# Adding up a paired tile's seven products in PSUM, with two of the four weight sums and the right factors' sums moved from GpSimd to VectorE

## The chip, the core and the metric

The kernel runs on one core of one Trainium2 chip. The metric is device time in microseconds (us): the median of several executions of the same program. Five engines share the work: TensorE (PE in the profile; its weight loads are PEld), VectorE (DVE), ScalarE (ACT), GpSimd (POOL) and SyncE (SP), which issues the DMAs. Each engine works through its own queue in order; semaphores tie the queues together. Matrix products land in PSUM, in eight banks; everything else lives in SBUF.

## What is computed

One decoder layer for 512 prompt tokens and 32 sample tokens, T = 544 columns in all: a half-step SwiGLU feed-forward block, a mixer (block-sparse attention and a gated linear recurrence side by side), and a second half-step SwiGLU block. The change touches the two feed-forward blocks.

```python
x = x + 0.5 * swiglu(rms_norm(x, ffn1_norm), ffn1_gate, ffn1_up, ffn1_down)
h = rms_norm(x, mix_norm); z = h @ w_in          # split among head groups
x = x + concat(moba(q, k, v), gate * norm(hgrn2(q, f, i))) @ w_out
x = x + 0.5 * swiglu(rms_norm(x, ffn2_norm), ffn2_gate, ffn2_up, ffn2_down)
```

Here swiglu(x) = (silu(x @ gate) * (x @ up)) @ down, with 1024 model columns and 2816 hidden columns.

## The kernel before

**Layout.** Activations are kept transposed: eight tiles `x[0..7]` of 128 model columns by 544 tokens. `HT` = 272 is half of the tokens, and every large matrix product is 128 by 128 by 272. Each operand is split into a high part, a cast to the format that TensorE takes at full pace (fp32r), and a low part, the remainder; a product is three matmuls, high by high, high by low and low by high (`products`). So every weight tile costs an ACT cast (`whi`) and a DVE subtraction (`wlo`), which `split_unit` issues. When a raw slot or a slot for split weights is taken from elsewhere, these appear under names such as `xh` and `xl`.

**Stages.** A feed-forward block has 22 hidden tiles in three groups (`FGROUPS`: 8, 8 and 6). For each group `ffn` first makes the hidden tiles and then adds their share of the down projection, eight output tiles. Below they are called groups A, B and C.

**Plain and paired tiles.** The first `NREG` = 4 hidden tiles are plain: gate and up are two products each over eight k-tiles and two token halves, 96 matmuls per hidden tile. They read `xg`, which needs no norm factor `R`, so that they can start early. From the fifth tile on, gate and up are made together. The four quarters of their weights (a11, a12: gate, first and second half of k; a21, a22: up) and the four quarters of the normed activations are combined by Winograd's form of Strassen's scheme: seven products instead of eight, 84 matmuls per hidden tile. It needs

- four weight sums per tile, S0 = a21 + a22, S1 = S0 - a11, S2 = a11 - a21, S3 = a12 - S1, which `w_split` issues on POOL,
- seven right factors per k-pair (`right_factors`, run as a side chain once per block as soon as `R` exists): two products on DVE, four sums of 272 columns on POOL, and four splits on ACT and DVE,
- the results added up from the seven products. `paired_gemm` gives each product its own bank out of three (`mm`), and `hidden_paired` takes them in: two are copied by ACT (`s1`, `s5`, in the tile `t_g`), five are added to an SBUF operand by DVE (into `sq`, `t_s`, `t_h`), and two further sums of SBUF operands go to POOL (`late`). ACT applies silu twice; one DVE product over 544 columns and the split of the hidden tile (`hh`, `hl`) end the tile.

**What sets the order.** The whole program is planned before anything is emitted. `Order` keeps a model of each engine's time; the backbone (the PE stream) and side chains are generators, and every instruction gets a planned start. `fit` puts an instruction of DVE, ACT or POOL into the first free gap of that engine's modelled time, also behind the current moment, and each engine's queue is then emitted in the order of planned starts (`give_out`). The durations in `cost` are a rough model; the real ones come from the trace.

**Weights.** `w_pump` splits weight tiles as long as a slot is free, and loads raw tiles as long as a raw slot is free. `next_w` hands units to the PE stream in the order in which they were split, which for a paired tile is a11, S0, S1, S2, a12, S3, a22. Four slots of each kind always exist; during the paired tiles `more_slots` lends four more raw and six more split ones.

Of the kernel before, what the change touches and what calls it, by code (L numbers as in the profile page):

```python
# [14 lines left out]
AF = mybir.ActivationFunctionType  # L15
ALU = mybir.AluOpType
# [11 lines left out]
HT = T // 2  # L28
# [22 lines left out]
OVER, TICK, WARM_COLUMNS = 0.0112, 3.413, 3060  # L51
NREG = 4
WARM = 10
# [123 lines left out]
class Engine:  # L177
# [22 lines left out]
    def __getattr__(self, op):  # L200
        real = getattr(self.real, op)

        def call(*args, **kw):
            names = list(self.tensors(args, kw))
            if op == "dma_start":
                s = self.order.dma(self.part, 4 * args[1].shape[0] * self.free(args[1]), names)
            elif op == "indirect_dma_start":
                s = self.order.dma(self.part, 4 * args[0].shape[0] * self.free(args[0]),
                                   names + [args[3].ap.tensor.name], 1.0)
            else:  # L210
                s = self.order.spend(self.part, self.cost(op, args, kw), names, op)
            self.order.note(s, real, args, kw)

        return call

    def cost(self, op, args, kw):
# [27 lines left out]
class Order:  # L244
# [4 lines left out]
    def __init__(self):  # L249
        self.free = {"pe": 0.0}  # L250
        self.busy = {part: [] for part in ("dve", "act", "pool", "sp", "dma")}
        self.written, self.touched, self.slots, self.work, self.before = {}, {}, {}, {}, {}
# [35 lines left out]

    def fit(self, part, s, cost):

        q = self.busy[part]
        if len(q) > 400:
            del q[:200]
        if q:
            s = max(s, q[0][0])
        i = len(q)
        while i and q[i - 1][1] > s:
            i -= 1
        while i < len(q) and q[i][0] < s + cost:
            s = max(s, q[i][1])  # L300
            i += 1
        q.insert(i, (s, s + cost))
        return s
# [11 lines left out]

    def spend(self, part, cost, names, op):
        s = self.start(part, names)
# [75 lines left out]
class Build:  # L393
# [123 lines left out]
    def w_split(self):  # L517
# [10 lines left out]
        if job["paired"]:  # L528
            (a11, a12, a21, a22) = (r for r, _ in job["raw"])
            if n == 0:  # L530
                S = [self.tl(self.sums, [128, 4, 128], f"S{i}") for i in range(4)]
                for i, (p, q, op) in enumerate(((a21, a22, ALU.add), (S[0], a11, ALU.subtract),
                                                (a11, a21, ALU.subtract), (a12, S[1], ALU.subtract))):
                    self.nc.gpsimd.tensor_tensor(S[i][:, :nk], p[:, :nk], q[:, :nk], op=op)
                job["units"] = (a11, S[0], S[1], S[2], a12, S[3], a22)
            src = job["units"][n]
            self.units.append(self.split_unit(src, nk, x))
            drop = {0: (0, 2), 4: (1,), 6: (3,)}.get(n, ())
        else:
# [10 lines left out]
    def w_pump(self):  # L550
        while self.w_split() or self.w_load():
            pass
# [32 lines left out]

    def products(self, ps, w, k, xh, xl, first, last):
        hi, lo, _ = w
        for i, (ww, xx) in enumerate(((hi, xh), (hi, xl), (lo, xh))):
            self.nc.tensor.matmul(ps[:, :HT], ww[:, k], xx, start=first and i == 0, stop=last and i == 2)

# [28 lines left out]

    PAIRED = (0, 3, 4, 5, 1, 2, 6)  # L620

    def paired_gemm(self, xw, nk, evacs):


        for r, evac in zip(self.PAIRED, evacs):
            w, = self.next_w(1)
            ps = self.mm()
            for k in range(nk):
                xh, xl = xw[k]
                self.products(ps, w, k, xh[:, r], xl[:, r], k == 0, k == nk - 1)  # L630
                yield
            evac(ps[:, :HT])
            self.free_w([w])

    def right_factors(self, pool, x, gain):
# [6 lines left out]

        def pace(t):
            self.order.t = self.order.free["pe"] + t

        def split(hi, lo, r, src):
            nc.scalar.copy(hi[:, r], src)
            nc.vector.tensor_tensor(lo[:, r], src, hi[:, r].bitcast(F32), op=ALU.subtract)

        for k in range(n):  # L650
# [4 lines left out]
            lo = self.tl(pool, [128, 7, HT], f"xwl{k}", F32R)  # L655
            for B, m in ((B1, k), (B2, k + n)):
                nc.vector.scalar_tensor_tensor(B.rearrange("p a b -> p (a b)"), x[m],
                                               self.gains[:, gain, m:m + 1], self.R, op0=ALU.mult, op1=ALU.mult)
                pace(1.2)
# [4 lines left out]
            split(hi, lo, slice(0, 1), B1[:, 0:1])  # L664
            pace(1.2)
            yield
            split(hi, lo, slice(1, 3), B2)
            pace(1.2)
            yield
            split(hi, lo, slice(3, 5), S1)  # L670
            pace(1.2)
            yield
            split(hi, lo, slice(5, 7), S2)
            self.xw.append((hi, lo))
            pace(1.2)
            yield

# [107 lines left out]
    def hidden_paired(self, pool, i, hs):  # L785
# [6 lines left out]
        l, r = self.cols(0), self.cols(1)  # L792
        s1, s5, u2, u3 = p[:, l], p[:, r], q[:, l], q[:, r]
        add = lambda out, x, y: nc.vector.tensor_tensor(out, x, y, op=ALU.add)
        late = lambda out, x, y: nc.gpsimd.tensor_tensor(out, x, y, op=ALU.add)
# [9 lines left out]
        def p2(x):  # L805
            add(s[:, l], x, s1)
            nc.scalar.activation(s[:, l], s[:, l], AF.Silu)

        def p3(x):
            add(s[:, r], x, s[:, r])  # L810
            nc.scalar.activation(s[:, r], s[:, r], AF.Silu)

        def p4(x):
            add(u[:, l], x, u3)
            nc.vector.tensor_tensor(u, u, s, op=ALU.mult)
            hs[i] = self.split_hidden(u, i)

        return lambda x: nc.scalar.copy(s1, x), lambda x: nc.scalar.copy(s5, x), p6, p7, p2, p3, p4


# [140 lines left out]
    def load_x(self, pool, p, x):  # L961
# [17 lines left out]
        self.loading = self.splitting = 0  # L979
        self.units = []  # L980
        self.slots = {"raw": [{"pool": self.wp, "tags": ("raw",), "bufs": 4, "used": 0, "freed": [], "extra": None}],
                      "w": [{"pool": self.wp, "tags": ("whi", "wlo"), "bufs": 4, "used": 0, "freed": [], "extra": None}]}
# [851 lines left out]
```

## Time and profile before

| | us |
|---|---|
| median of 3 executions | 1233.71 |
| lowest, highest | 1231.61, 1234.82 |
| the profiled execution's own time | 1229.04 |
| its span, first to last instruction | 1227.3 |

| stretch of the profiled span | from, to (us) |
|---|---|
| start, plain tiles of the first block | 0 to 73.2 |
| first block: paired tiles of groups A, B, C | 73.2 to 127.8, 177.9 to 270.0, 317.8 to 382.5 |
| mixer | about 382 to 838 |
| second block: plain tiles | about 838 to 883.8 |
| second block: paired tiles of groups A, B, C | 883.8 to 933.5, 981.3 to 1069.7, 1117.6 to 1182.3 |
| last down projection and output | to the end |

How to read the profile: a row of the windows view gives a stretch, its length, and then for each engine how long it was busy and with how many instructions, and the granted share of TensorE's clock (PEclk). A row of the timeline gives the start and the length of an instruction, then its engine, operation and tiles (out<-in), shapes and, in square brackets, the idle time of the engine before it and what ended that. All instructions are recorded by one helper, so every row names the same line of the code (L274); the tiles tell them apart. Durations of neighbours on one engine overlap slightly, since the next one starts while the last is draining; the distance from start to start is what a queue pays.

### The profile page before, as it was taken

How to read it: one execution, taken by the hardware profiler on the slowest of the kernel's cores; microseconds unless marked ns; L12 is line 12 of the kernel's file. 1: busy time of each engine (PE TensorE's matmuls, PEld its weight loads, DVE VectorE, ACT ScalarE, POOL GpSimd, SP SyncE). 2: the span in 40 equal slices, each digit the busy share in tenths (PEclk: the TensorE clock that was granted, in tenths of full speed). 3: DMA queues.
4: the chain of work that ended last, by engine and by line, in shares of the span. 5: the costliest groups of instructions: out<-in, count | busy, mean ns of one | idle time of the engine just before them, and what ended most of it. 6: DMA issues, size and time to landing. Idle time of an engine off the chain costs nothing. (4 is left out here: it accounts for less than half of the span.)

```text
span 1227.3 us, 26588 instructions
## 1 busy us (share of the span) xinstructions
PE 1184.0 (96%) x10547; PEld 1114.1 (91%) x10547; DVE 911.0 (74%) x1671; ACT 544.0 (44%) x1103; POOL 473.3 (39%) x391
## 2 busy tenths in 40 slices
PE   8969999999999999999999999899889999999998
PEld 8969998999999998888878877799889999999998
DVE  6999649993796678888777457668897499937953
ACT  5445324542454426554556432344453255514532
POOL 3367118750662331000233344122573277505710
PEclk8999999999999999999999999899999999999999
DMA  5233353242313551432565786332433323332222
GB/s 161 73 105 99 107 160 96 85 118 82 89 55 98 169 181 56 129 87 70 182 193 166 231 275 234 132 111 71 119 98 110 95 79 95 110 89 78 65 84 81
DMA packets 216239, 144.74 MB, mean 118 GB/s; under 512 B 12035, under 2 KB 204067, under 8 KB 216116
## 3 DMA queue, kind: packets, MB, share of 16 engines
q1 hardware_dynamic: 205588, 106.60, 30.1%
q0 software_dynamic: 10432, 36.32, 9.0%
q8 instruction: 83, 1.36, 0.4%
q14 instruction: 40, 0.33, 0.1%
q10 hardware_dynamic: 96, 0.14, 0.0%
HBM read 133.94 MB, written 11.83 MB: 119 GB/s over the span
## 5 line engine op out<-in xcount | busy, mean ns | idle before, releaser
L274 PE MATMUL mm<-xh,whi 128*128 128x272 f32 x1152 | 346.4, 301 | 1.5 <-ACT xh L274 1.0
L274 PE MATMUL mm<-xh,wlo 128*128 128x272 f32 x1152 | 334.1, 290 | 5.0 <-DVE wlo L274 5.0
L274 PE MATMUL mm<-xl,whi 128*128 128x272 f32 x1152 | 333.9, 290 | 5.0 <-DVE xl L274 4.9
L274 ACT CAST whi<-raw 128x512 fp32r<-128x512 f32 (+1 forms) x224 | 135.3, 605 | 241.4 <-PE mm L274 182.9
L274 PEld LDWEIGHTS mm<-xh,whi 128*128 128x128 f32 x1152 | 218.8, 190 | 18.7 <-issue 16.0
L274 DVE TENSOR_TENSOR wlo<-raw,whi 128x512 fp32r<-128x512 f32 (+1 forms) x224 | 172.0, 775 | 73.5 <-ACT whi L274 69.7
L274 PEld LDWEIGHTS mm<-xl,whi 128*128 128x128 f32 x1152 | 219.3, 190 | 6.2 <-DVE xl L274 6.1
L274 PEld LDWEIGHTS mm<-xh,wlo 128*128 128x128 f32 x1152 | 218.9, 190 | 6.1 <-DVE wlo L274 6.1
L274 PE MATMUL mm<-xwh,xh 128*128 128x272 f32 x624 | 184.3, 295 | 10.8 <-DVE sq L274 7.8
L274 PE MATMUL mm<-xwl,xh 128*128 128x272 f32 x624 | 181.4, 291 | 0.0
L274 PE MATMUL mm<-xwh,xl 128*128 128x272 f32 x624 | 181.4, 291 | 0.0
L274 PEld LDWEIGHTS mm<-xwh,xh 128*128 128x128 f32 x624 | 119.4, 191 | 15.8 <-DVE sq L274 10.1
L274 PEld LDWEIGHTS mm<-xwl,xh 128*128 128x128 f32 x624 | 119.4, 191 | 0.0
L274 PEld LDWEIGHTS mm<-xwh,xl 128*128 128x128 f32 x624 | 119.2, 191 | 0.0
L274 PE MATMUL mm<-xwh,whi 128*128 128x272 f32 x384 | 112.4, 293 | 5.9 <-ACT t_g L274 2.7
L274 POOL TENSOR_TENSOR S<-raw,raw 128x512 f32<-128x512 f32 x28 | 42.0, 1500 | 189.5 <-DMA raw<-ffn_up 184.2
L274 PE MATMUL mm<-xwh,wlo 128*128 128x272 f32 x384 | 110.6, 288 | 3.1 <-DVE wlo L274 3.1
L274 PE MATMUL mm<-xwl,whi 128*128 128x272 f32 x384 | 110.3, 287 | 0.0
L274 PE MATMUL mm<-hl,whi 128*128 128x272 f32 x352 | 101.4, 288 | 0.0
L274 PE MATMUL mm<-hh,whi 128*128 128x272 f32 x352 | 101.2, 288 | 0.0
L274 PE MATMUL mm<-hh,wlo 128*128 128x272 f32 x352 | 101.2, 288 | 0.0
L274 DVE TENSOR_TENSOR xl<-S,xh 128x512 fp32r<-128x512 f32 x88 | 94.5, 1075 | 4.0 <-ACT xh L274 2.6
(308 smaller groups left out, 2439.4 us busy)
## 6 DMA issues: line engine op xcount, KB each, us to landing
raw<-ffn_down SPq DMA_DIRECT2D x64, 256.0 KB, 2.8
raw<-ffn_up SPq DMA_DIRECT2D x60, 256.0 KB, 3.0
raw<-w_in SPq DMA_DIRECT2D x56, 256.0 KB, 3.1
raw<-ffn_gate SPq DMA_DIRECT2D x48, 256.0 KB, 3.2
xh<-ffn_gate SPq DMA_DIRECT2D x24, 256.0 KB
raw<-ffn_down SPq DMA_DIRECT2D x32, 192.0 KB, 2.5
xl<-ffn_up SPq DMA_DIRECT2D x18, 256.0 KB, 2.9
xl<-ffn_gate SPq DMA_DIRECT2D x16, 256.0 KB, 3.3
```

Of the source, the lines that this page charges most:

```text
L274: call(*map(real, args), **{k: real(v) for k, v in kw.items()})
```

## The change

**Sums in PSUM.** A paired tile now owns three banks a, b and d, alternately from the `mm` and the `sm` banks (`self.turn`). The first three products open the three banks; the other four are added by TensorE onto what is there (`start=False` throughout). Between them VectorE adds `s1` to bank b in place. In order:

1. P1 into a; ACT copies it to `s1`
2. P6 into b; DVE adds `s1` to b in PSUM, ACT copies the result to `u2`
3. P5 into d; ACT copies it to `s5`
4. P2 onto a; ACT applies silu straight from the bank
5. P7 onto b; DVE writes b + `s5` to the right half of `t_h`
6. P3 onto d; DVE adds `u2`, ACT applies silu, DVE multiplies the right half (272 columns) of `t_h`
7. P4 onto b; DVE multiplies it with the left silu, and the hidden tile is split

The four additions that VectorE made on the way are now two (to b, and of `u2`) plus one (`s5`); the two sums on POOL are gone.

**Sums moved.** S0 and S1 go from POOL to DVE, S2 and S3 stay; the units' order becomes a11, S1, S0, a12, S2, S3, a22. In `right_factors` all four sums per k-pair go from POOL to DVE, each as a step of its own with a pause of 0.8 in the planner's time (`PACE`).

**Planner.** `NREG` is 5: one more tile is plain. A weight tile is split only while fewer than `AHEAD` = 4 are waiting at that point of the plan. DVE instructions with two larger SBUF operands and all POOL instructions but memsets now also reserve a common resource `port` in the plan.

```diff
-NREG = 4
+NREG = 5
+AHEAD = 4
+PACE = 0.8
...
+    def shares_port(self, op, args, kw):
+        if self.part not in ("dve", "pool") or op == "memset":
+            return False
+        n = sum(hasattr(x, "tensor") and self.free(x) > 1 and x.tensor.name[:2] not in ("mm", "sm")
+                for x in args[1:] if hasattr(x, "shape"))
+        return self.part == "pool" or n > 1
...
-            s = self.fit(part, s, cost)
+            s = self.fit([part, "port"] if port else part, s, cost)
...
-                for i, (p, q, op) in enumerate(((a21, a22, ALU.add), (S[0], a11, ALU.subtract),
-                                                (a11, a21, ALU.subtract), (a12, S[1], ALU.subtract))):
-                    self.nc.gpsimd.tensor_tensor(S[i][:, :nk], p[:, :nk], q[:, :nk], op=op)
-                job["units"] = (a11, S[0], S[1], S[2], a12, S[3], a22)
+                for i, (e, p, q, op) in enumerate(((self.nc.vector, a21, a22, ALU.add),
+                                                   (self.nc.vector, S[0], a11, ALU.subtract),
+                                                   (self.nc.gpsimd, a11, a21, ALU.subtract),
+                                                   (self.nc.gpsimd, a12, S[1], ALU.subtract))):
+                    e.tensor_tensor(S[i][:, :nk], p[:, :nk], q[:, :nk], op=op)
+                job["units"] = (a11, S[1], S[0], a12, S[2], S[3], a22)
...
-        while self.w_split() or self.w_load():
+        while (len(self.units) < AHEAD and self.w_split()) or self.w_load():
...
-    PAIRED = (0, 3, 4, 5, 1, 2, 6)
+    PAIRED = ((0, 0, True), (1, 4, True), (2, 3, True), (0, 1, False), (1, 5, False), (2, 2, False), (1, 6, False))
...
-        for r, evac in zip(self.PAIRED, evacs):
+        self.turn = not self.turn
+        ps = [self.mm() if self.turn else self.sm() for _ in range(3)]
+        views = [p[:, :HT] for p in ps]
+        for (b, r, first), evac in zip(self.PAIRED, evacs):
             w, = self.next_w(1)
-            ps = self.mm()
             for k in range(nk):
                 xh, xl = xw[k]
-                self.products(ps, w, k, xh[:, r], xl[:, r], k == 0, k == nk - 1)
+                self.products(ps[b], w, k, xh[:, r], xl[:, r], first and k == 0, k == nk - 1, not first)
                 yield
-            evac(ps[:, :HT])
+            evac(*views)
             self.free_w([w])
...
-            for out, p, q in ((S1[:, 0], B1[:, 1], B1[:, 0]), (S1[:, 1], B2[:, 1], S1[:, 0]),
-                              (S2[:, 0], B2[:, 1], B1[:, 1]), (S2[:, 1], B2[:, 0], S1[:, 1])):
-                nc.gpsimd.tensor_tensor(out, p, q, op=ALU.subtract)
...
+            steps += [lambda a=a: diff(*a) for a in ((S1[:, 0], B1[:, 1], B1[:, 0]), (S1[:, 1], B2[:, 1], S1[:, 0]),
+                                                     (S2[:, 0], B2[:, 1], B1[:, 1]), (S2[:, 1], B2[:, 0], S1[:, 1]))]
...
+            for step in steps:
+                step()
+                self.order.t = self.order.free["pe"] + PACE
                 yield
...
-        def p6(x):
-            add(u2, x, s1)
-            late(s[:, r], u2, s5)
-
-        def p7(x):
-            add(u3, x, u2)
-            late(u[:, r], u3, s5)
...
+        def p6(a, b, d):
+            add(b, b, s1)
+            nc.scalar.copy(u2, b)
+
+        def p3(a, b, d):
+            add(g, d, u2)
+            silu(s[:, r], g)
+            nc.vector.tensor_tensor(u[:, r], u[:, r], s[:, r], op=ALU.mult)
+
+        def p4(a, b, d):
+            nc.vector.tensor_tensor(u[:, l], b, s[:, l], op=ALU.mult)
             hs[i] = self.split_hidden(u, i)
...
+        return (lambda a, b, d: nc.scalar.copy(s1, a), p6, lambda a, b, d: nc.scalar.copy(s5, d),
+                lambda a, b, d: silu(s[:, l], a), lambda a, b, d: add(u[:, r], b, s5), p3, p4)
```

**What moves on VectorE.** The rows below are VectorE's queue in the fourth paired tile of group B of the first block, before: one tile's worth of rows from the sum of P6 (`sq` from a bank `mm` and `t_g`) on. A row is an operation, out<-in and its shape; `xl` and `wlo` from a raw tile or an `S` are weight remainders, `hl` is that of the hidden tile.

```order
L274 TENSOR_TENSOR sq_515_2744<-mm_2718,t_g_2700 128x272
L274 TENSOR_TENSOR xl_525_2755<-S_499_2628,xh_524_2741 128x512
L274 TENSOR_TENSOR sq_515_2744<-mm_2738,sq_515_2744 128x272
L274 TENSOR_TENSOR xl_528_2775<-raw_2475,xh_527_2766 128x512
L274 TENSOR_TENSOR t_s_2753<-mm_2763,t_g_2700 128x272
L274 TENSOR_TENSOR xl_536_2798<-raw_2439,xh_535_2790 128x512
L274 TENSOR_TENSOR t_s_2753<-mm_2787,t_s_2753 128x272
L274 TENSOR_TENSOR wlo_2819<-S_531_2672,whi_2811 128x512
L274 TENSOR_TENSOR t_h_2773<-mm_2808,sq_515_2744 128x272
L274 TENSOR_TENSOR t_h_2773<-t_h_2773,t_s_2753 128x544
L274 TENSOR_TENSOR wlo_2845<-S_532_2703,whi_2832 128x512
L274 TENSOR_TENSOR hl_544_2860<-t_h_2773,hh_543_2848 128x544
```

The same tile after the change, from the addition into bank b on:

```order
L284 TENSOR_TENSOR mm_2637<-mm_2637,t_g_2641 128x272
L284 TENSOR_TENSOR xl_484_2667<-xl_414_2275,xh_483_2647 128x512
L284 TENSOR_TENSOR xl_494_2676<-S_471_2565,xh_493_2661 128x512
L284 TENSOR_TENSOR S_500_2686<-raw_2530,raw_2593 128x512
L284 TENSOR_TENSOR xl_496_2697<-S_472_2590,xh_495_2690 128x512
L284 TENSOR_TENSOR S_501_2706<-S_500_2686,raw_2435 128x512
L284 TENSOR_TENSOR t_h_2726<-mm_2637,t_g_2641 128x272
L284 TENSOR_TENSOR xl_498_2730<-xh_437_2444,xh_497_2710 128x512
L284 TENSOR_TENSOR sq_458_2670<-mm_2658,sq_458_2670 128x272
L284 TENSOR_TENSOR t_h_2726<-t_h_2726,t_s_2704 128x272
L284 TENSOR_TENSOR t_h_2726<-mm_2637,t_s_2704 128x272
L284 TENSOR_TENSOR xl_505_2771<-raw_2435,xh_504_2723 128x512
```

The next tile's two weight sums (`S_500`, `S_501`) now stand in VectorE's queue just ahead of the row that reads bank b after the fifth product (`t_h` from `mm` and `t_g`); the row that multiplies `t_h` by the second silu follows right behind the row that feeds that silu (`sq`).

**What moves on GpSimd.** Its queue for one tile there before (the sums of the next tile, and the two sums `t_s` and `t_h` of this one):

```order
L274 TENSOR_TENSOR S_496_2517<-xh_452_2436,raw_2475 128x512
L274 TENSOR_TENSOR S_497_2548<-S_496_2517,xh_432_2341 128x512
L274 TENSOR_TENSOR S_498_2572<-xh_432_2341,xh_452_2436 128x512
L274 TENSOR_TENSOR t_s_2598<-sq_480_2589,t_g_2545 128x272
L274 TENSOR_TENSOR t_h_2618<-sq_480_2589,t_g_2545 128x272
L274 TENSOR_TENSOR S_499_2628<-xl_433_2278,S_497_2548 128x512
```

and after, for three tiles in a row:

```order
L284 TENSOR_TENSOR S_471_2565<-xh_413_2334,xl_423_2381 128x512
L284 TENSOR_TENSOR S_472_2590<-xl_414_2275,S_470_2557 128x512
L284 TENSOR_TENSOR S_502_2714<-raw_2435,raw_2530 128x512
L284 TENSOR_TENSOR S_503_2739<-raw_2483,S_501_2706 128x512
L284 TENSOR_TENSOR S_533_2863<-xh_475_2632,xl_485_2679 128x512
L284 TENSOR_TENSOR S_534_2888<-xl_476_2584,S_532_2855 128x512
```

Six rows per tile have become two.

More of the change, by code (lines that the diff above doesn't have):

```diff
@@ L210, in call @@
             else:
-                s = self.order.spend(self.part, self.cost(op, args, kw), names, op)
+                s = self.order.spend(self.part, self.cost(op, args, kw), names, op, self.shares_port(op, args, kw))
             self.order.note(s, real, args, kw)
         return call
+    def shares_port(self, op, args, kw):
[4 more added lines that the diff above has]
+        return self.part == "pool" or n > 1
     def cost(self, op, args, kw):
@@ L250, in __init__ @@
         self.free = {"pe": 0.0}
-        self.busy = {part: [] for part in ("dve", "act", "pool", "sp", "dma")}
+        self.busy = {part: [] for part in ("dve", "act", "pool", "sp", "dma", "port")}
         self.written, self.touched, self.slots, self.work, self.before = {}, {}, {}, {}, {}
@@ L287, in born, with fit @@
         q.append(name)
[L289 to L302, printed above, removed]
+    def fit(self, parts, s, cost):
+        parts = [parts] if isinstance(parts, str) else parts
+        for part in parts:
+            q = self.busy[part]
+            if len(q) > 400:
+                del q[:200]
+            if q:
+                s = max(s, q[0][0])
+        while True:
+            first, at = s, []
+            for part in parts:
+                q = self.busy[part]
+                i = len(q)
+                while i and q[i - 1][1] > s:
+                    i -= 1
+                while i < len(q) and q[i][0] < s + cost:
+                    s = max(s, q[i][1])
+                    i += 1
+                at.append((q, i))
+            if s == first or len(parts) == 1:
+                break
+        for q, i in at:
+            q.insert(i, (s, s + cost))
         return s
@@ L314, in start, with spend @@
         return s
-    def spend(self, part, cost, names, op):
+    def spend(self, part, cost, names, op, port=False):
         s = self.start(part, names)
@@ L584, in first_weights, with products @@
         return w, load, split
-    def products(self, ps, w, k, xh, xl, first, last):
+    def products(self, ps, w, k, xh, xl, first, last, onto=False):
         hi, lo, _ = w
+        kw = {"skip_group_check": True} if onto else {}
         for i, (ww, xx) in enumerate(((hi, xh), (hi, xl), (lo, xh))):
-            self.nc.tensor.matmul(ps[:, :HT], ww[:, k], xx, start=first and i == 0, stop=last and i == 2)
+            self.nc.tensor.matmul(ps[:, :HT], ww[:, k], xx, start=first and i == 0, stop=last and i == 2, **kw)
     def gemm_unit(self, ps, h, w, nk, k, x, first, last):
@@ L641, in right_factors, with lows, diff @@
         n = KD // 2
-        def pace(t):
-            self.order.t = self.order.free["pe"] + t
-        def split(hi, lo, r, src):
+        def lows(hi, lo, r, src):
             nc.scalar.copy(hi[:, r], src)
             nc.vector.tensor_tensor(lo[:, r], src, hi[:, r].bitcast(F32), op=ALU.subtract)
+        def diff(out, p, q):
+            nc.vector.tensor_tensor(out, p, q, op=ALU.subtract)
         for k in range(n):
@@ L792, in hidden_paired @@
         l, r = self.cols(0), self.cols(1)
-        s1, s5, u2, u3 = p[:, l], p[:, r], q[:, l], q[:, r]
+        s1, s5, u2, g = p[:, l], p[:, r], q[:, l], q[:, r]
         add = lambda out, x, y: nc.vector.tensor_tensor(out, x, y, op=ALU.add)
-        late = lambda out, x, y: nc.gpsimd.tensor_tensor(out, x, y, op=ALU.add)
-        def p6(x):
-            add(u2, x, s1)
-            late(s[:, r], u2, s5)
-        def p7(x):
-            add(u3, x, u2)
-            late(u[:, r], u3, s5)
[L805 to L815, printed above, removed]
+        silu = lambda out, x: nc.scalar.activation(out, x, AF.Silu)
+        def p6(a, b, d):
[7 more added lines that the diff above has]
+            nc.vector.tensor_tensor(u[:, l], b, s[:, l], op=ALU.mult)
             hs[i] = self.split_hidden(u, i)
-        return lambda x: nc.scalar.copy(s1, x), lambda x: nc.scalar.copy(s5, x), p6, p7, p2, p3, p4
+        return (lambda a, b, d: nc.scalar.copy(s1, a), p6, lambda a, b, d: nc.scalar.copy(s5, d),
+                lambda a, b, d: silu(s[:, l], a), lambda a, b, d: add(u[:, r], b, s5), p3, p4)
     def ffn(self, pool, wide, home, x, xg, done, first=None):
```

24 lines of the change are left out of this document (7 added, 17 removed).

## The prediction

> **What bounds the kernel now.** I read the page's busy shares first, then who waits for whom, then the windows of the six stretches of paired tiles.
>
> ```profile
> PE 1184.0 (96%) x10547; PEld 1114.1 (91%) x10547; DVE 911.0 (74%) x1671; ACT 544.0 (44%) x1103; POOL 473.3 (39%) x391
> ...
> PE mm L274 <- DVE sq L274: 9.3, 8, 3.1
> PE mm L274 <- DVE wlo L274: 8.1, 8, 1.9
> PE mm L274 <- ACT t_g L274: 5.7, 9, 2.1
> PE mm L274 <- DVE xl L274: 4.9, 3, 3.6
> ```
>
> PE sets the time, and what it waits for in products is mostly VectorE: sums out of PSUM (`sq`), weight remainders (`wlo`), and ACT's copies out of PSUM (`t_g`). Where:
>
> ```profile
> 269.80:318.00 48.20, 48.20 (x388) 48.20 (x387) 20.82 (x36) 10.65 (x18) 5.96 (x5) 1.00 0.30 89
> ...
> core 0: us, PE busy (x) PEld busy (x) DVE busy (x) ACT busy (x) POOL busy (x), PEclk, DMA share, GB/s
> 73.20:127.80 54.60, 46.88 (x339) 45.10 (x339) 51.43 (x64) 27.93 (x54) 40.67 (x28) 0.94 0.44 119
> 177.90:270.00 92.10, 87.51 (x676) 84.96 (x675) 86.58 (x110) 48.70 (x98) 69.00 (x48) 1.00 0.34 98
> 317.80:382.50 64.70, 64.30 (x507) 63.39 (x506) 55.52 (x77) 32.47 (x66) 39.62 (x28) 1.00 0.23 66
> 883.80:933.50 49.70, 44.91 (x340) 43.93 (x339) 47.12 (x61) 26.77 (x52) 35.33 (x25) 0.97 0.46 132
> 981.30:1069.70 88.40, 86.52 (x675) 84.79 (x674) 84.47 (x110) 47.18 (x95) 64.03 (x44) 1.00 0.34 96
> 1117.60:1182.30 64.70, 64.21 (x508) 63.48 (x507) 55.40 (x77) 32.43 (x66) 39.02 (x28) 1.00 0.23 66
> sum 414.20, PE 394.33 PEld 385.63 DVE 380.50 ACT 215.47 POOL 287.66; mean PE 65.72 PEld 64.27 DVE 63.42 ACT 35.91 POOL 47.94
> ```
>
> The first row is a down projection with nothing in PE's way: 8 x 2 x 8 x 3 = 384 matmuls in 48.20 us, 0.1255 us each. At that pace a paired tile (84 matmuls) takes 10.54 us and a plain one (96) 12.05. The 36 paired tiles take 414.20, or 11.51 each, against 379.4 at full pace. So 34.8 us are lost there, 14.1 of them because the four tiles of each group A cost more than those of group B (54.60 - 4 x 11.51 = 8.6 and 49.70 - 4 x 11.05 = 5.5). In groups A and B VectorE is busy 94 to 96% of the time: the paired tiles run at VectorE's pace. Why it is slow, its own queue tells:
>
> ```profile
> 87.29 1.28 DVE L274 TENSOR_TENSOR xl<-S,xh 128x512 fp32r<-128x512 f32 x2
> 88.49 0.43 DVE L274 TENSOR_TENSOR sq<-mm,t_g 128x272 f32<-128x272 f32 x1
> 88.84 0.68 DVE L274 TENSOR_TENSOR wlo<-S,whi 128x512 fp32r<-128x512 f32 x1
> 89.44 1.27 DVE L274 TENSOR_TENSOR wlo<-raw,whi 128x512 fp32r<-128x512 f32 x1
> ...
> 44.06 0.73 DVE L274 TENSOR_TENSOR hl<-t_h,hh 128x544 fp32r<-128x544 f32 x1
> 44.70 0.72 DVE L274 TENSOR_TENSOR t_s<-t_s,R 128x544 f32<-128x544 f32 x1
> 59.48 0.43 DVE L274 TENSOR_TENSOR xwl<-hh,xwh 128x272 fp32r<-128x272 f32 x1
> 59.83 0.43 DVE L274 TENSOR_TENSOR t_h<-mm,t_s 128x272 f32<-128x272 f32 x1
> ...
> 195.30 1.66 DVE L274 TENSOR_TENSOR wlo<-S,whi 128x512 fp32r<-128x512 f32 x1
> 196.89 1.78 DVE L274 TENSOR_TENSOR wlo<-xh,whi 128x512 fp32r<-128x512 f32 x1
> 198.59 0.43 DVE L274 TENSOR_TENSOR sq<-mm,t_g 128x272 f32<-128x272 f32 x1
> ...
> 195.12 1.30 POOL L274 TENSOR_TENSOR S<-raw,raw 128x512 f32<-128x512 f32 x1 [1.91 <-DMA raw<-ffn_up]
> 196.49 1.63 POOL L274 TENSOR_TENSOR S<-S,raw 128x512 f32<-128x512 f32 x1
> ```
>
> From start to start a remainder of 512 columns costs 0.60 (two from 87.29 to 88.49), one of 544 columns 0.64, a sum out of PSUM 0.35 (88.49 to 88.84), and 272 columns of SBUF operands 0.35. But beside a sum on POOL the same remainder costs 1.70 (196.89 to 198.59): it ends some 0.55 after POOL's sum, which ends at 198.12. So POOL's sums hold VectorE up, and VectorE holds PE up.
>
> **The change, part by part.**
>
> *A paired tile on VectorE.* Before, by the rows in the section on the change: 7 remainders (4.20), 5 sums out of PSUM (1.75), a product and a remainder of 544 columns (1.28), together 7.23. The windows show 86.58 / 8 = 10.82 in the first block's group B and 84.47 / 8 = 10.56 in the second's. The difference, 3.59 and 3.33, is hold-up by POOL, which is busy 69.00 / 8 = 8.63 and 64.03 / 8 = 8.00 there: 42% of POOL's busy time. After: 7 remainders (4.20), 2 weight sums of the same width (not shown on VectorE before; the nearest row is the remainder of 512 columns, 1.20 for two; bounds 0.70 from 272 columns and 3.40 from held-up ones), 4 operations on PSUM (1.40), a product of 272 columns (0.35) and `hl` (0.64): 7.79. POOL keeps two sums of about 1.6 (196.49), 3.2 in all, and at 42% they hold VectorE up for 1.34. That share is my choice; its bounds are 0 and the whole 3.2. Busy: 9.1.
>
> The sum into bank b in place, PSUM to PSUM, no row shows; I take the 0.35 of a sum into SBUF. Between nothing and twice that, the total moves by 0.35, less than the room found below.
>
> *Idle time of VectorE.* Before it was (92.10 - 86.58) / 8 = 0.69 and (88.40 - 84.47) / 8 = 0.49 per tile, partly for PE; I keep 0.4. New is a wait in the middle of the queue: the product of `t_h` with the second silu stands right behind the sum that feeds that silu.
>
> ```profile
> 201.46 0.43 DVE L274 TENSOR_TENSOR t_s<-mm,t_g 128x272 f32<-128x272 f32 x1
> ...
> 201.92 0.43 ACT L274 ACTIVATE t_s<-t_s 128x272 f32<-128x272 f32 x1 [3.25 <-DVE t_s L274]
> ```
>
> ACT starts 0.03 after the sum's end and takes 0.43, so VectorE stands for about 0.5. Behind it are the product of the left half and the next remainders, which have a lead. Together 9.1 + 0.4 + 0.5 = 10.0 per tile, under PE's 10.54: **PE takes the pace back**, with half a microsecond to spare.
>
> *New waits of PE.* It comes back to a bank two products (3.0 us) after leaving it, once after only one (1.5 us): the seventh product waits until VectorE has read b after the fifth. That read takes 0.43, but a weight sum held up by POOL, up to 1.7, can be in front of it; then PE loses up to 0.6. Averaged over tiles I charge 0.1. The two-product turns need at most a sum and a copy, 0.43 + 0.4, and have 2 us of room. A tile: 10.65.
>
> *ACT* gets a third copy (0.4) and is busy 48.70 / 8 = 6.1 of 11.5 before: hidden behind PE's 10.5. If that cover were gone, the copy of `u2` would be late for bank b, the same wait as above.
>
> *One more plain tile per block*: two tiles at 12.05, no longer paired.
>
> *Before the first pairs.*
>
> ```profile
> 36.00:73.20 37.20, 33.84 (x253) 32.98 (x252) 35.77 (x54) 19.88 (x34) 18.20 (x17) 0.95 0.26 71
> 838.00:883.80 45.80, 43.74 (x346) 43.30 (x347) 39.77 (x61) 23.04 (x40) 22.15 (x20) 1.00 0.24 70
> ```
>
> VectorE is full here in the first block (35.77 of 37.20). It gets 16 sums of 272 columns, 5.6 us, but 12 more microseconds to do them in, and most of POOL's 18.20 beside it goes. Of the 8.1 that PE waits for `wlo` I let 3 go. The costly starts of groups A come from the same backlog, and from the clock, which fell after the longest waits:
>
> ```profile
> 88.97 0.40 PE L274 MATMUL mm<-xwh,xh 128*128 128x272 f32 x1 [3.11 <-DVE sq L274]
> 92.11 0.43 PE L274 MATMUL mm<-xwl,xh 128*128 128x272 f32 x1
> ```
>
> (0.43 in place of 0.29, and PEclk 0.94 in that stretch.) I keep half of the 14.1: 7.
>
> *Sum.* 34 x 10.65 + 2 x 12.05 + 7 = 393.2 against 414.2: -21; with the 3 from the plain tiles -24. The profiled execution took 1229.04, of it 1227.3 its span, and becomes 1205. It stands 4.7 below the median of the runs, so I subtract from the median: 1233.7 - 24 = **1210**. The mixer's queues are also planned anew with the same instructions; I take nothing for it, and its longest single wait (`xl`, 3.6) as a bound on either side.
>
> **The rivals.** The break-even is (414.2 - 24.1) / 34 = 11.47 us per paired tile, starts included; 0.3% (3.7 us), about what a measurement of this kernel can tell from no change, lies 0.11 further.
>
> *PE unhindered.* Tiles at 10.54 and no lost starts: 358.4 + 24.1 = 382.5, -31.7, and -5 before the pairs: 1197. For it: the groups C, at 10.78 before. Against it: VectorE's queue at the starts.
>
> *POOL's sums are paid in full.* If each of the two left costs VectorE its 1.30 in full, a tile takes 7.79 + 2.6 + 0.9 = 11.3, and VectorE keeps the pace: 384.2 + 24.1 + 7 = 415.3, +1, less 3: 1232, no change. For it: the row at 196.89. Against it: only 42% was paid before, since POOL also ran beside sums out of PSUM and idle time; one of the two sums left starts just when `S_501` ends, and the next row reads PSUM. The Trainium skill (page "SBUF — State Buffer", section "SBUF: two separate sides") says that a VectorE instruction with two SBUF inputs and a GpSimd one hold a port pair exclusively, so that the loser "fully blocks". The row at 196.89 agrees; that rule at every meeting gives this rival's 1232, and the share of the windows gives 1210.
>
> *Slower: the weight sums wait for their weights on VectorE.* POOL waited 1.91 for a raw tile at 195.12, and nobody minded. Now S0 stands on VectorE ahead of the read of bank b: if it waits, PE waits for b. At 1.91 per tile: 10.0 + 1.9 = 11.9, 404.6 + 31.1 = 435.7, +21.5, less 3: 1252. It decides from 1.6 per tile on. Against it:
>
> ```profile
> raw<-ffn_up SPq DMA_DIRECT2D x60, 256.0 KB, 3.0
> ```
>
> a load lands 3.0 after its issue, and the raw slot that the last quarter needs comes free at the remainder `xl_498`, ten VectorE rows (some 6 us) before the next tile's sum.
>
> **How the numbers follow.** Forecast, 1200 to 1222: 0.60. PE unhindered, under 1200: 0.12. Sums paid in full, 1222 to 1236: 0.18, half of it still faster by over 0.3% (under 1230.0). Slower by over 0.3% (over 1237.4), by late weights or a longer wait for bank b: 0.10. So faster 0.80, within 0.3% 0.10, slower 0.10. The range 1197 to 1233 leaves out the slower case, the upper end of the second rival and a little below: under 2 in 10.
>
> **What would show it.** Right: POOL's busy time in a group B falls to some 25 of 85 us, VectorE's remainders beside no POOL sum at 0.68, the windows of group B at 84 to 87 us, PE's waits for `sq`, `t_g` and `wlo` under 10 together. Wrong: the windows of group B still near 90 with VectorE over 95% busy (sums paid in full), idle time of VectorE before `S` ended by a DMA (late weights), or PE waiting for `t_h`, at the seventh product, in most tiles (bank b).

## The result and the profile after

The changed kernel takes 1211.43 us (median of 4 runs, 1210.65 to 1211.78) where the kernel before takes 1233.1 (4 runs, 1231.61 to 1234.82): a ratio of 0.9823, with a 95% interval of 0.9806 to 0.9840. Its profiled execution took 1210.65, of it 1208.9 its span.

The page's busy shares, and from the list of waits what TensorE waited for (us in all, times, longest):

```profile
PE 1178.1 (97%) x10571; PEld 1113.7 (92%) x10571; DVE 858.5 (71%) x1729; ACT 551.9 (46%) x1125; POOL 228.3 (19%) x211
```

```profile
PE mm L284 <- DVE xl L284: 5.2, 3, 3.1
PE sm L284 <- DVE kn L284: 4.1, 3, 3.2
...
PE mm L284 <- DVE t_h L284: 1.4, 4, 0.8
PE sm L284 <- DVE t_h L284: 1.3, 1, 1.3
PE mm L284 <- DVE wlo L284: 1.1, 2, 0.6
```

POOL's busy time has more than halved (473.3 before). The waits for `sq`, `wlo` and `t_g` that led the list, 23.1 together, are down to little; new is a wait for `kn`, which belongs to the mixer. The windows of the paired stretches (columns as in the prediction):

```profile
81.40:115.70 34.30, 32.70 (x255) 31.82 (x254) 29.95 (x48) 21.17 (x46) 9.21 (x7) 1.00 0.47 130
166.50:251.40 84.90, 84.90 (x675) 84.30 (x674) 77.14 (x118) 52.16 (x105) 22.50 (x15) 1.00 0.38 109
299.40:362.40 63.00, 63.00 (x506) 63.00 (x505) 49.72 (x80) 35.36 (x72) 11.48 (x8) 1.00 0.23 67
886.60:919.80 33.20, 31.93 (x255) 31.71 (x254) 29.10 (x46) 20.18 (x43) 7.95 (x6) 1.00 0.44 128
967.90:1052.20 84.30, 84.30 (x674) 84.30 (x674) 71.31 (x115) 51.76 (x103) 23.66 (x14) 1.00 0.35 101
1100.30:1163.40 63.10, 63.10 (x506) 63.10 (x505) 47.98 (x80) 35.51 (x72) 13.12 (x8) 1.00 0.23 67
```

In both groups B and both groups C TensorE is busy for the whole window: 295.3 us for 28 tiles, 10.55 each, its own pace. VectorE was the full engine before (94 to 96%); now it has room. Outside the paired tiles, the start, and the mixer after and before:

```profile
0.00:81.40 81.40, 75.87 (x561) 72.89 (x562) 65.23 (x124) 41.88 (x72) 12.94 (x20) 0.98 0.42 113
...
362.40:830.00 467.60, 450.90 (x4843) 394.23 (x4841) 332.64 (x825) 211.18 (x475) 114.14 (x124) 0.98 0.49 152
```

```profile
382.50:838.00 455.50, 446.21 (x4844) 390.16 (x4842) 329.21 (x825) 211.27 (x476) 115.82 (x124) 0.99 0.50 156
```

The mixer, in which no instruction was changed, is 12 us longer. With every stretch cut at its first matmul (worked out from the trace, so the windows' rounding is gone), the profiled executions differ like this:

| stretch | before | after | difference | predicted |
|---|---|---|---|---|
| paired tiles (36, then 34) and the two tiles that became plain (24.1) | 413.4 | 362.6 + 24.1 | -26.7 | -21 |
| starts and plain tiles of both blocks, without those two | 119.0 | 137.9 - 24.1 | -5.2 | -3 |
| mixer, with the down projection of group C ahead of it | 455.6 | 467.8 | +12.2 | 0 |
| four down projections (groups A and B), end | 239.3 | 240.5 | +1.2 | 0 |
| span | 1227.3 | 1208.9 | -18.4 | -24 |

### The profile page after: what moved, and what is told of

It is laid out like the page before. It is cut to its first block, busy times and chain, and to the rows that moved or that the text cites. A ratio compares the mean times of both kernels' runs of the same rounds, so it can differ in the third digit from the quotient of the medians.

```text
span 1208.9 us, 26320 instructions
## 1 busy us (share of the span) xinstructions
PE 1178.1 (97%) x10571; PEld 1113.7 (92%) x10571; DVE 858.5 (71%) x1729; ACT 551.9 (46%) x1125; POOL 228.3 (19%) x211
## 4 chain that ended last, share of the span: by engine, by line
PE 77%; DVE 13%; ACT 3%; DMA 3%; issue 2%; SPq 1%; POOL 0%; DVEq 0%; ACTq 0%; POOLq 0%
PE mm L284 51%; PE sm L284 26%; DVE wlo L284 3%; DVE xl L284 2%; DVE xwl L284 1%; DMA raw<-ffn_down 1%; ACT xh L284 1%; DVE t_h L284 1%; SPq L284 1%; ACT whi L284 1%; DVE hl L284 1%; ACT sq L284 1%; DMA raw<-ffn_up 1%; DVE S L284 1%; DMA KV<-cache_v,idx 1%
## 5 line engine op out<-in xcount | busy, mean ns | idle before, releaser
L284 PE MATMUL mm<-xwh,xh 128*128 128x272 f32 x296 | 85.4, 288 | 1.3 <-DVE t_h L284 0.8
L284 PE MATMUL sm<-xwl,xh 128*128 128x272 f32 x296 | 85.3, 288 | 0.0
L284 PE MATMUL mm<-xwl,xh 128*128 128x272 f32 x296 | 85.3, 288 | 0.0
L284 PE MATMUL sm<-xwh,xh 128*128 128x272 f32 x296 | 85.2, 288 | 0.0
L284 PE MATMUL mm<-xwh,xl 128*128 128x272 f32 x296 | 85.2, 288 | 0.0
L284 PE MATMUL sm<-xwh,xl 128*128 128x272 f32 x296 | 85.2, 288 | 0.0
L284 DVE TENSOR_TENSOR xl<-S,xh 128x512 fp32r<-128x512 f32 x84 | 66.0, 796 | 4.1 <-ACT xh L284 3.7
L284 PEld LDWEIGHTS mm<-hh,whi 128*128 128x128 f32 x352 | 66.3, 188 | 0.7 <-ACT whi L284 0.5
L284 ACT CAST xh<-S 128x512 fp32r<-128x512 f32 x84 | 51.8, 620 | 32.7 <-DVE S L284 13.7
L284 PEld LDWEIGHTS mm<-hh,wlo 128*128 128x128 f32 x352 | 66.2, 188 | 0.0
```

What stands on the lines that cost most here:

```text
L284: call(*map(real, args), **{k: real(v) for k, v in kw.items()})
```

## The experiments

Each was timed beside the kernel before on the same chip; that kernel took between 1228.15 and 1229.27 there, so the ratios are what compares. The lengths of stretches come from the profiled execution of each, cut as in the table.

### What each part of the gain is worth

**The weight sums back on POOL.** The change, with S0 and S1 where they were.

```diff
-for i, (e, p, q, op) in enumerate(((self.nc.vector, a21, a22, ALU.add),
-                                   (self.nc.vector, S[0], a11, ALU.subtract),
+for i, (e, p, q, op) in enumerate(((self.nc.gpsimd, a21, a22, ALU.add),
+                                   (self.nc.gpsimd, S[0], a11, ALU.subtract),
```

> S0 and S1 go back to GpSimd (four weight sums there), all else as after the change. By the prediction's terms (42% of GpSimd's busy time holds VectorE up): VectorE 7.79 - 1.20 + 0.42 x 6.4 + 0.9 = 10.2 us per paired tile, still under TensorE's 10.54: the windows of group B stay at 84 to 86, total 1210 to 1215, so that moving them was worth nothing by itself. Rival (each sum on GpSimd is paid in full, 1.30): 6.59 + 5.2 + 0.9 = 12.7 per tile, group B over 95, total over 1260.

Measured: 1221.34, ratio 0.9931 [0.9906, 0.9955]. The paired stretches take 377.1, 14.5 more than in the change; the groups B 87.7 and 87.8, between the two expectations. One place of the second group B on VectorE, its window, and the row on TensorE behind it:

```profile
1000.52 1.78 DVE L284 TENSOR_TENSOR xl<-S,xh 128x512 fp32r<-128x512 f32 x1
1002.23 1.77 DVE L284 TENSOR_TENSOR wlo<-S,whi 128x512 fp32r<-128x512 f32 x1
1003.92 0.43 DVE L284 TENSOR_TENSOR t_h<-mm,t_g 128x272 f32<-128x272 f32 x1
...
973.40:1061.20 87.80, 85.00 (x674) 84.35 (x673) 71.15 (x97) 48.80 (x102) 42.26 (x28) 1.00 0.30 87
```

```profile
1004.40 0.39 PE L284 MATMUL mm<-xwh,xh 128*128 128x272 f32 x1 [0.77 <-DVE t_h L284]
```

VectorE is busy 71 of 87.8 us, yet two remainders that POOL's sums hold to 1.7 us each stand ahead of the read of bank b, and TensorE stops for it. In each group B TensorE stops for that read twice, for 0.8 and 1.8 us, and that is nearly all of the 2.8 it is idle there. So what the sums on POOL cost here is no longer throughput: it is a delay in front of a short turn. It is the wait that the prediction named for bank b and put at up to 0.6; with remainders held in front it is 0.77 at this place and 1.79 at the other. Of the 14.5, 6.1 lie in the groups A, 6.4 in the groups B and 2.1 in the groups C (each rounded).

**The products apart again.** Each product in its own `mm` bank, five additions on VectorE and two on POOL as before; sums, order of weights and the sixth-tile start as in the change.

```diff
-        ps = [self.mm() if self.turn else self.sm() for _ in range(3)]
         for (b, r, first), evac in zip(self.PAIRED, evacs):
             w, = self.next_w(1)
+            ps = self.mm()
...
-            add(b, b, s1)
-            nc.scalar.copy(u2, b)
+            add(u2, x, s1)
...
+            late(u[:, r], u3, s5)
```

> The adding in PSUM is undone: each product has its own bank, VectorE adds five of them and GpSimd makes the two late sums, as before; the units' order and the moved sums stay. By the prediction's terms: VectorE 7.23 + 1.20 + 0.42 x 5.6 + 0.4 = 11.2 per paired tile, over TensorE's 10.54 by 0.65: group B at 88 to 91 us, total about 1211 + 34 x 0.65 = 1233. Rival (the moved sums alone freed VectorE): group B at 84 to 86, total 1210 to 1214.

Measured: 1218.46, ratio 0.9912 [0.9895, 0.9928]; paired stretches 374.1, 11.5 more than in the change. The groups B, 88.3 each, are as expected; the total is lower than expected, since the groups A lost nothing (34.3 and 32.7) and the groups B and C lost 0.47 and 0.36 per tile in place of 0.65. In the paired stretches TensorE then waits for weight remainders alone, 7.6 for `xl` and 4.5 for `wlo`; the first rows of the list for the whole program:

```profile
PE mm L284 <- DVE xl L284: 12.1, 11, 3.6
PE mm L284 <- DVE wlo L284: 5.6, 9, 0.8
```

Undoing the sums' move loses 14.5 of the 26.7 that the paired stretches gained, undoing the accumulation 11.5. That the two nearly add up is no proof that they are independent: the planner's limit, below, is worth as much again. Nor is the 11.5 the additions' alone, since this version also brings back two sums on POOL; the next experiment adds such two to the change.

**More sums on POOL.** The change, with two additions of 272 columns per tile on POOL whose results nobody reads.

```diff
+        def p5(a, b, d):
+            nc.scalar.copy(s5, d)
+            nc.gpsimd.tensor_tensor(s1, u2, s5, op=ALU.add)
+        def p7(a, b, d):
+            add(u[:, r], b, s5)
+            nc.gpsimd.tensor_tensor(s1, u2, s5, op=ALU.add)
```

> Two sums of 272 columns per paired tile are added on GpSimd, whose results nobody reads, as the two late sums were before. Theory (GpSimd's sums hold VectorE up, and VectorE then holds TensorE up): GpSimd's busy time per tile in group B rises from 2.9 to about 5.3 us, hold-up per tile from 1.1-1.8 to about 2.4, VectorE's need to 7.79 + 2.4 + 0.9 = 11.1 against TensorE's 10.54: paired stretches 34 x 0.5 = 17 us longer, 375 to 382 in all, group B at 87 to 90. Rival (what counts is only VectorE's own number of operations): paired stretches unchanged, 362 to 365.

Measured: 1213.33, ratio 0.9888 [0.9866, 0.9909]; paired stretches 368.1, 6.0 more than in the change timed again on that chip (362.1), nearer to the rival than to the theory.

```profile
167.70:254.20 86.50, 85.06 (x674) 84.18 (x673) 73.43 (x112) 50.38 (x102) 37.40 (x30) 1.00 0.32 92
```

POOL is busy 37.40 in place of 24.15 and the group B is 2 us longer, yet VectorE is busy no longer than before (73.43; 75.93 in the change on that chip). A part of that is work that has moved: 6 or 7 of VectorE's rows now run in the down projection behind the group. But row by row, too, it is held up no more: 1.69 and 1.45 per tile in the two groups B, against 1.57 and 1.61 in the change on that chip and 2.4 in the theory. The groups C did not move (63.0). So POOL's sums cost by where they fall, not in proportion to their time.

**The limit on split weights, the fifth tile, the factors' sums.** These three start from the best version below ("the second silu's wait filled": paired stretches 359.7, first stretch and group A 114.2).

```diff
-AHEAD = 4
+AHEAD = 99
```

> On the kernel of the silu edit: no limit to the number of weight tiles split ahead. If the limit only changes the order of the plan and not who is late, paired stretches stay at 359 to 362 and the total at 1193 to 1197. Rival (unlimited splitting puts casts that wait for a slot ahead of ScalarE's copies out of PSUM, as the waits for the copies before the change suggest): waits of TensorE for ScalarE's copies come back, paired stretches 365 or more.

Measured: 1211.73, ratio 0.9867 [0.9851, 0.9884]; paired stretches 374.5, 14.8 more, nearly all of it in the groups A:

```profile
81.30:121.50 40.20, 34.33 (x254) 33.27 (x253) 31.76 (x49) 22.53 (x46) 10.53 (x7) 0.96 0.49 133
881.40:920.60 39.20, 33.44 (x254) 33.01 (x253) 32.65 (x49) 21.87 (x44) 8.89 (x6) 0.96 0.44 127
```

33.4 and 31.9 with the limit; the groups B and C do not notice it. The time is the rival's, but its cause is so only in part: without the limit TensorE waits once for 4.0 us for VectorE's `t_h` in each group A, and 1.9 and 1.7 for ScalarE's copies. The mean granted clock is 0.96 there.

```diff
-NREG = 5
+NREG = 4
```

> On the kernel of the silu edit: pairs again from the fifth tile on (four plain tiles). TensorE has 24 matmuls less, 3.0 us. If the sixth-tile start was needed, because VectorE is full before the first pairs (right factors, their sums and five tiles' remainders), the stretch from the start to the end of the first group A gives those 1.5 us back or more and the total is 1194 to 1199; if it was not, the total is 1190 to 1192.

Measured: 1200.51, ratio 0.9779 [0.9763, 0.9796], above both expectations. In the first block the start and the group A take 121.1 in place of 114.2, though a paired tile has 1.5 us less of matmuls than a plain one; in the second block 88.2 against 88.5.

```profile
68.30:121.10 52.80, 45.98 (x337) 45.40 (x338) 45.54 (x74) 29.76 (x60) 11.17 (x8) 0.90 0.37 96
```

In this window TensorE waits 3.4 for ACT's copy of `u2` (`sq`) and 3.4 for a `wlo`, and the clock is 0.90: ACT and VectorE are still behind. The extra plain tile pays for itself in the first block alone.

```diff
         def diff(out, p, q):
-            nc.vector.tensor_tensor(out, p, q, op=ALU.subtract)
+            nc.gpsimd.tensor_tensor(out, p, q, op=ALU.subtract)
```

> On the kernel of the silu edit: the four sums per k-pair of the right factors go back to GpSimd. VectorE has 16 x 0.35 = 5.6 us less per block but is held up by 16 sums of about 1.1 us. By the 42% that is 7.4 us of hold-up per block: first stretch and first group A together 1 to 3 us longer (114.2 before this edit), total 1194 to 1198. Rival (full payment, 17.6 us per block): 8 us or more longer there.

Measured: 1196.9, ratio 0.9746 [0.9725, 0.9768]; start and group A 115.5 in place of 114.2, as expected. The time alone can't tell it from 1194.22: the intervals overlap.

### Why the mixer got longer

**The change again**, on another chip, to see whether the long mixer belongs to the kernel.

> The changed kernel as it is, on the chip of the runs beside it, so that these can be compared with it: 1206 to 1213 us, paired stretches 362 to 364 us in all, mixer 466 to 469.

Measured: 1205.96, ratio 0.9815 [0.9797, 0.9833]; mixer 465.6. It does.

**No reservation of the port in the plan.**

```diff
-        if self.part not in ("dve", "pool") or op == "memset":
+        if True:
             return False
```

> Leaves everything of the change but the planner's reservation of the port: the mixer's TensorE queue is then the one of before again, row for row. Theory A (the 12 us that the mixer lost come from its new order, which the reservation made): mixer stretch back to 455 to 458 us from 467.6, total 1198 to 1203. Rival B (the mixer lost them otherwise, for example since its gathers and weight loads start at other times): mixer stays at 465 to 469, total 1210 to 1214. Either way group B in 84 to 88 us if the hold-up of VectorE by GpSimd does not hang on the reservation; over 90 if it does.

**Reservation in the feed-forward blocks alone** (`port_on` is cleared where the mixer begins and set where the second block does).

```diff
-        if self.part not in ("dve", "pool") or op == "memset":
+        if not self.order.port_on or self.part not in ("dve", "pool") or op == "memset":
             return False
```

> The reservation holds only while the feed-forward blocks are planned, the mixer is planned without it. Theory A: mixer 455 to 458, paired stretches as after the change, total 1198 to 1201, the best of these. Rival B: total 1210 to 1213.

Measured: 1201.86, ratio 0.9781 [0.9765, 0.9798], without any reservation, and 1197.7, ratio 0.9741 [0.9725, 0.9758], with it in the feed-forward blocks alone. Their mixers, in this order:

```profile
364.50:818.20 453.70, 445.04 (x4845) 388.88 (x4843) 329.50 (x825) 210.98 (x476) 115.31 (x124) 0.99 0.51 156
```

```profile
362.30:816.50 454.20, 444.52 (x4844) 388.50 (x4842) 327.82 (x825) 210.96 (x476) 115.29 (x124) 1.00 0.51 156
```

Both are back at the length of before. In the feed-forward blocks the reservation is worth 2.0 (paired stretches 364.7 without, 362.7 with, one profiled execution each). So the 12 us come from the order that the reservation leads to in the mixer. One place shows how: VectorE's queue around 530 us, then POOL's, TensorE's and a window, in the change:

```profile
527.95 2.65 DVE L284 TENSOR_TENSOR wlo<-raw,whi 128x512 fp32r<-128x512 f32 x2
530.62 0.74 DVE L284 SCALAR_TENSOR_TENSOR kn<-sm,qkg,kn 64x512 fp32r<-64x512 f32 x1
...
528.28 1.77 POOL L284 TENSOR_TENSOR kt<-kt,gkrow 128x640 f32<-128x640 f32 x1 [32.41 <-PE sm L284]
...
528.83 0.37 PE L284 MATMUL mm<-xh,whi 128*128 128x272 f32 x1
...
533.02 0.55 PE L284 MATMUL sm<-kn,qh 128*128 128x256 f32 x1 [3.19 <-DVE kn L284]
...
531.60:541.80 10.20, 8.78 (x29) 7.03 (x30) 7.12 (x22) 3.82 (x11) 0.00 (x0) 0.50 0.28 79
```

and the same work with the reservation in the feed-forward blocks alone:

```profile
522.24 1.28 DVE L285 TENSOR_TENSOR wlo<-raw,whi 128x512 fp32r<-128x512 f32 x2
...
524.72 0.74 DVE L285 SCALAR_TENSOR_TENSOR kn<-sm,qkg,kn 64x512 fp32r<-64x512 f32 x1
...
524.23 1.57 POOL L285 TENSOR_TENSOR kt<-kt,gkrow 128x640 f32<-128x640 f32 x1 [32.19 <-PE sm L285]
...
524.17 0.40 PE L285 MATMUL mm<-xh,whi 128*128 128x272 f32 x1
...
527.30 0.28 PE L285 MATMUL sm<-kn,qh 128*128 128x256 f32 x1
```

There the two remainders run ahead of POOL's `kt`, in 1.28, and `kn` is ready before TensorE needs it. In the change they stand ahead of `kn` and beside `kt`, take 2.65, and TensorE waits 3.19; the granted clock falls to 0.50 inside that wait and stays there for 10.2 us.

The held remainders, 1.37 longer, are the smaller cause of that wait. The larger is TensorE's own queue: between the matmuls on `y_qk` and the first on `kn` it has 6 matmuls of a projection in the change (from 528.83) and 24 in the other version (from 524.17), 18 x 0.1255 = 2.3 us less to fill the time with. The executions agree on it: in all five with a long mixer (the change twice, the sums back, the products apart, more sums on POOL) 3 or 6 matmuls stand there and TensorE waits 3.2 to 3.6; in all with a short one 24 stand there and it does not wait.

Over the whole mixer TensorE's idle time rises from 9.3 to 16.7 and the time at half clock from 10.2 to 20.5. By an estimate that half of the 10.2 more is lost, this is 7.5 + 5.1 = 12.6, against 12.2 measured; for the change timed again it gives 3.6 + 8.5 = 12.1 against 10.0, so the division between the two is rough.

**The kernel before, with the reservation in the mixer alone.**

```diff
-                s = self.order.spend(self.part, self.cost(op, args, kw), names, op)
+                s = self.order.spend(self.part, self.cost(op, args, kw), names, op, self.shares_port(op, args, kw))
...
+        self.order.port_on = True
         with self.pool("mix") as mp:
```

> The kernel before, with nothing of the change but the planner's reservation, and that in the mixer alone. If reserving makes a worse order there, the mixer gets longer than 455.6, towards 468, and the feed-forward blocks stay as before (paired stretches 413): total 5 to 13 us above before. Rival (the loss needs the changed feed-forward blocks around it): mixer 454 to 457, total within 2 us of before.

Measured: 1227.48 (10 runs), ratio 0.9994 [0.9984, 1.0004]; mixer:

```profile
382.30:837.00 454.70, 443.36 (x4845) 389.01 (x4843) 331.57 (x825) 210.66 (x476) 113.93 (x124) 0.99 0.51 156
```

The reservation in the mixer does no harm by itself. It does harm together with what the change leaves behind when the mixer begins. The mixer stays long, 463.6 and 464.9, with the weight sums back on POOL and with the products apart, so neither of these two parts by itself is needed for it; which of the others (the plain tile, the limit on split weights, the factors' sums, the order of the weights) tips the plan was not tried and stays open.

### A better version

**The second silu's wait filled.** The reservation in the feed-forward blocks alone, and the product with the second silu moved behind the product of the left half.

```diff
             silu(s[:, r], g)
-            nc.vector.tensor_tensor(u[:, r], u[:, r], s[:, r], op=ALU.mult)
 
         def p4(a, b, d):
             nc.vector.tensor_tensor(u[:, l], b, s[:, l], op=ALU.mult)
+            nc.vector.tensor_tensor(u[:, r], u[:, r], s[:, r], op=ALU.mult)
```

> On the kernel that reserves in the feed-forward blocks only: VectorE's product with the second silu moves behind the product of the left half, so that a weight remainder fills the 0.5 us in which VectorE stood still for that silu. If TensorE has the pace and VectorE half a microsecond to spare, nothing is gained: paired stretches 361 to 364 (362.7 before this edit), total within 2 us of 1197.7. If VectorE still decides in many tiles, up to 0.4 us per tile goes: 350s are impossible, but the 4.3 us over TensorE's own 358.4 should vanish, 358 to 360.

Measured: 1194.22 (5 runs), ratio 0.9727 [0.9711, 0.9743], the lowest ratio of all, though its interval overlaps that without this edit (0.9725 to 0.9758); the gain is read from the paired stretches. VectorE now goes on after the sum that feeds the silu, and the sum row of the six paired windows follows:

```profile
982.42 0.43 DVE L285 TENSOR_TENSOR sq<-mm,sq 128x272 f32<-128x272 f32 x1
982.77 0.68 DVE L285 TENSOR_TENSOR wlo<-xh,whi 128x512 fp32r<-128x512 f32 x1
983.38 0.44 DVE L285 TENSOR_TENSOR t_h<-mm,t_s 128x272 f32<-128x272 f32 x1
...
sum 359.70, PE 358.58 PEld 357.71 DVE 308.13 ACT 220.56 POOL 83.46; mean PE 59.76 PEld 59.62 DVE 51.35 ACT 36.76 POOL 13.91
```

34 tiles at 10.54 are 358.4: only 1.3 us is left in the paired tiles without fewer matmuls. The wait was worth 3.0 (362.7 with it), 1.7 of it in the groups A and 1.2 in the groups B (each rounded).

## Why the prediction was right, and where it was not

The forecast of 1210 against 1211.43 is better than its terms, and that it came so close is luck. Two of them, the paired stretches and the mixer, were off in opposite directions, and the profile of before, 4.1 below its median where that of after is 0.8 below, made up the rest: -18.4 between the profiles, -21.7 between the medians.

**VectorE's work per tile: right.** One tile of the second group B after the change, VectorE and then POOL:

```profile
992.39 0.44 DVE L284 TENSOR_TENSOR mm<-mm,t_g 128x272 f32<-128x272 f32 x1
992.74 0.68 DVE L284 TENSOR_TENSOR xl<-raw,xh 128x512 fp32r<-128x512 f32 x1
...
993.94 0.68 DVE L284 TENSOR_TENSOR S<-xl,xh 128x512 f32<-128x512 f32 x1
994.60 1.74 DVE L284 TENSOR_TENSOR wlo<-S,whi 128x512 fp32r<-128x512 f32 x1
996.26 0.68 DVE L284 TENSOR_TENSOR S<-S,xh 128x512 f32<-128x512 f32 x1
996.86 0.43 DVE L284 TENSOR_TENSOR t_h<-mm,t_g 128x272 f32<-128x272 f32 x1
997.21 1.70 DVE L284 TENSOR_TENSOR wlo<-raw,whi 128x512 fp32r<-128x512 f32 x1
998.84 0.43 DVE L284 TENSOR_TENSOR sq<-mm,sq 128x272 f32<-128x272 f32 x1
999.76 0.44 DVE L284 TENSOR_TENSOR t_h<-t_h,t_s 128x272 f32<-128x272 f32 x1 [0.50 <-ACT t_s L284]
```

```profile
994.10 1.68 POOL L284 TENSOR_TENSOR S<-xh,xl 128x512 f32<-128x512 f32 x1 [6.46 <-DVE xl L284]
997.07 1.30 POOL L284 TENSOR_TENSOR S<-xl,S 128x512 f32<-128x512 f32 x1 [1.28 <-DMA raw<-ffn_up]
```

The sum into bank b in place costs 0.35 from start to start (992.39 to 992.74), as taken. The weight sum on VectorE costs 0.60 (996.26 to 996.86), the value of the nearest row. POOL's two sums meet a remainder each, which takes 1.7. Adding up every row's excess over its undisturbed length, the hold-up is 1.77 and 1.05 per tile in the two groups B (1.57 and 1.61 when the change was timed again); 1.34 was predicted. Without it the windows leave 77.14 / 8 - 1.77 = 7.87 and 71.31 / 8 - 1.05 = 7.86, against 7.79. The silu's wait is 0.50 where it was put:

```profile
DVE t_h L284 <- ACT t_s L284: 4.0, 8, 0.5
```

(VectorE's waits in one group B: once in each of eight tiles.)

**TensorE takes the pace back: right**, groups B at 84.90 and 84.30, inside the 84 to 87 that was given, with POOL busy 22.50 and 23.66 (some 25 was given).

**The wait for bank b: mis-sized.** 0.1 per tile was charged; in the groups B and C TensorE never waits for it (10.55 per tile), and all 2.3 us of it in the paired stretches lie in the groups A. The experiment with the sums back on POOL shows the size it can have. **The starts: mis-sized**: 7 predicted, 4.1 measured (34.2 + 33.1 less 6 x 10.54). Of the 5.7 by which the paired stretches did better than predicted, 3.7 (34 tiles, 10.54 in place of 10.65) and 2.9 are these two, by rounded terms (the windows' edges, 0.8 in the 414.2, go the other way). **The plain tiles** gave 5.2 in place of 3.

**The mixer: wrong.** The prediction has its queues "planned anew with the same instructions; I take nothing for it", with the longest single wait, 3.6, as a bound. It cost 12.2. A single wait of the trace of before is no bound on an order that does not exist yet: the new order has a wait of 3.19 of its own, where TensorE's queue has 6 matmuls in place of 24 to run while `kn` is made, and 10.2 us at half clock begin in it.

**The rivals.** TensorE unhindered came nearly true in the feed-forward blocks; the mixer kept the change from that rival's time. The rival was -36.7; with the mixer as before the change gives -31.6 (1197.7 beside 1229.27), and with the silu's wait filled -33.9 (1194.22 beside 1228.15). POOL's sums paid in full would be 2.8 to 3.0 per tile, its busy time there; the groups B show 1.77 and 1.05. By the Trainium skill (page "SBUF — State Buffer", section "SBUF: two separate sides") whichever of the two starts first holds the port pair and the other blocks. The rows at 997.07 and 997.21 agree; the last section has a place that does not, where VectorE instructions that start after POOL's are not held. Late weights: VectorE never waited for a raw tile in the groups B, and once in a group A, 0.9 us. Bank b would have been the price, as the sums back on POOL show, had S0 and S1 stayed there.

## What to carry to other kernels

When two engines share a resource, count what is queued behind a held instruction before counting its time: sums on POOL cost TensorE nothing ahead of work with a lead, and a stop ahead of a bank that is needed next. When a planner's rule is added for one stage, apply it to that stage alone, and compare the other stages' windows, since a queue that is planned anew lost here 12.2 of the 31.9 that the other stages gained. Where a product is added onto its bank, the instruction that reads the bank in the middle sets the turn: keep ahead of it as little as possible that another engine can hold up. And when TensorE waits for a chain of other engines, look also at how many matmuls its own queue has to fill that time.

## What the runs showed of the hardware that was not expected

A POOL sum that comes second can be passed more than once. Here, in the change, it took 2.88, and VectorE's instructions beside it went on at 0.60 each, two of which started after POOL's:

```profile
1004.67 0.68 DVE L284 TENSOR_TENSOR S<-raw,raw 128x512 f32<-128x512 f32 x1
1005.27 0.68 DVE L284 TENSOR_TENSOR xl<-S,xh 128x512 fp32r<-128x512 f32 x1
1005.87 0.68 DVE L284 TENSOR_TENSOR S<-S,raw 128x512 f32<-128x512 f32 x1
...
1004.83 2.88 POOL L284 TENSOR_TENSOR S<-raw,raw 128x512 f32<-128x512 f32 x1 [6.46 <-DVE xl L284]
```

At 997.07, where POOL came first, its sum took 1.30 and the remainder behind it 1.70. At 994.10 it came second too, beside VectorE's sum of 993.94, but was passed by nothing: it took 1.68, and the next remainder was held, 1.74. What decides between the two cases is not shown. The share of POOL's time that VectorE pays was 42% before and 35% to 63% after, and is no constant.

Within a TensorE wait of 3.19 us in the mixer (529.8 to 533.0) began 10.2 us at a granted clock of 0.50. In the four other executions with that wait, 6.8 to 10.2 us at 0.50 began within it or up to 1.8 us behind it; without the wait the clock stayed at 1.00 there. If the clock fell for that wait, one late operand cost about 8 us, by the estimate above. The length of a wait does not tell alone: the paired stretches with waits of 2.0 to 4.0 show a mean clock of 0.90 to 0.97 and those without any 1.00, but one with a longest wait of 1.59 shows 0.96 and three with 1.8 show 1.00, and in the change 3.4 us at 0.50 began at 500.9 with no wait over 0.4 in the 30 us before.
